# A fourth block-sum step behind two down projections, and one rounding bound ahead of later weight halves

## The chip, the cores and the metric

The kernel runs on one core of one Trainium2 chip. The metric is the device time in microseconds (us), as the median of several runs. TensorE (PE) multiplies, VectorE (DVE) and ScalarE (ACT) round and add, GpSimd (POOL) and SyncE (SP) issue the transfers from HBM.

## The reference

A trunk of two residual layers over 256 tokens with 2048 features, all in float32. Layer 0 mixes with grouped-query attention, layer 1 with a gated recurrence; each is followed by the feed-forward stage that the change is in:

```python
def swiglu(h, w_gate, w_up, w_down):
    return (jax.nn.silu(h @ w_gate) * (h @ w_up)) @ w_down
...
        x = x + mix
        x = x + swiglu(rms_norm(x, norm_ffn[i]), ffn_w_gate[i], ffn_w_up[i], ffn_w_down[i])
```

`w_gate` and `w_up` have 5632 columns, `w_down` 5632 rows.

## The kernel before

*Rounded pairs.* Each operand is held as a rounded value `hi` and the rest `lo`, and a product of two is three matmuls (`hi*hi`, `hi*lo`, `lo*hi`). Weights come in halves of 128 x 1024 numbers: two blocks of 128 rows by 512 columns. For each half `load_half` issues the transfer on SP's queue, ScalarE casts `hi` (L141), and VectorE subtracts to get `lo` (L143). `raw` has 6 buffers, `hi` and `lo` have 5 each, so the rounding can run some five halves ahead of TensorE.

*Steps.* A pair of column groups (`j` = 0 and 1, 512 columns each) is multiplied by `project_pair` with all 16 blocks of the input, taken two at a time: eight steps `n` = 0 to 7. A plain step takes a half of weights for each column group, four products each, eight in all. A *block-sum step* (`seven_forms`) does the same 2 x 2 by 2 x 2 block product with seven products, from sums and differences of the blocks (the scheme of Strassen and Winograd). It needs the sums of the weights: SP loads `wx`, POOL's queue loads `sr` with two transfers, the second adding onto the first (two `sr` buffers, fetched two block sums ahead); VectorE adds (L320, L324, L325) and takes rests (L326, L328, L329), ScalarE casts (L322, L323, L327). `wx`, `wxh` and `wxl` have one buffer each. It also needs sums of the input blocks, the *forms* of `x_forms` (L338 to L343), made once for each block pair and kept. Four products gather in PSUM tiles `pm`; after the last block-sum step of a pair `merge` (L402 to L406) folds them into two tiles `g` and `u`, to which `done` adds the accumulators (four PSUM banks, `acc`).

*Plans.* `pair_plan` takes the first steps with both columns in turn, and the rest first for column 0 and then for column 1. `THREE` = steps 1, 3 and 5 are the block sums.

*The feed-forward stage.* The 44 tiles of hidden features are cut in parts of 12, 16 and 16 (`PARTS`). In each part *units* of four tiles are made one after the other (`unit`: column group 0 is the gate, 1 the up projection), units 0 to 2, 3 to 6 and 7 to 10 of a layer; behind each part stands its down projection (`down`), two pairs of column groups, of six or eight steps, which adds into `x_tok` (L586, L594). So units 3 and 7 come right behind a down projection.

*What a unit leaves.* Its result is turned on VectorE (L862), moved by sixteen small ScalarE copies (L868) and split into `hi` and `lo` tiles (L875, L876, `split_tiles`). This work is put in the list `owed`, and `settle` takes some of it at each step of the following pair, so that the last unit of a part is turned and split during the first steps of its down projection.

*Order.* TensorE's order is as written. The other engines' order is the planner's, with three bonds: `in_line` puts weight casts (ScalarE) and rests (VectorE) in the order of the halves; `follow` puts one instruction behind another of the same engine without a semaphore; `not_after(i)` makes the rest of the fourth weight half from there come behind `i`.

Of the kernel before, what the change touches and what calls it, by code (L numbers as in the profile page):

```python
# [12 lines left out]
F32 = mybir.dt.float32  # L13
F32R = mybir.dt.float32r
AF = mybir.ActivationFunctionType
ALU = mybir.AluOpType
# [5 lines left out]
KT = D // P  # L22
# [5 lines left out]
PARTS = [12, 16, 16]  # L28
THREE, TWO, SHORT = (1, 3, 5), (2, 5), 6
READY = 6  # L30
FIRST_STEPS = (0, 1, 2, 4, 3, 6, 5, 7)
HALF = 8
WIDE = 512
# [37 lines left out]
def trunk(ctx, tc, w, out):  # L71
# [26 lines left out]
    def follow(i, j):  # L98
        tc.add_manual_dep(
            i.ins, j.ins.name,  # L100
            mybir.DependencyInfo(mybir.DependencyClass.NoSync, mybir.DependencyReason.DATA),
            reason="order",
        )
        return i


    line = {}

    def in_line(eng, i):
        if eng in line:  # L110
            if line[eng] is not None:
                follow(i, line[eng])
            line[eng] = i
        return i
# [40 lines left out]
    def pair_plan(steps, together):  # L155
        return [(n, (0, 1)) for n in steps[:together]] + [(n, (j,)) for j in range(2) for n in steps[together:]]

    def unit_seven(i):
        return THREE

    def unit_plan(i):
        steps = range(KT // 2) if i else FIRST_STEPS
        return pair_plan(steps, 1 + steps.index(unit_seven(i)[-1]))

    def down_plan(n, alone):
        if alone:
# [164 lines left out]
        fetch_next()  # L331
        return [[t[:, k, :] for t in w] for w, k in ((w1, 0), (w1, 1), (w2, 0), (w2, 1), ((xh, xl), 0), ((xh, xl), 1), ((xh, xl), 2))]

    def x_forms(h0, h1, tag):
        y = fp[0].tile([P, 8, P], F32, tag="tb", name=nm("tb"))
        for i, h in enumerate((h0, h1)):
            o, hi, lo = y[:, 2 * i : 2 * i + 2, :].rearrange("p a t -> p (a t)"), h[:, :S].bitcast(F32), h[:, S:].bitcast(F32)
            dve.tensor_tensor(o, hi, lo, ALU.add)  # L338
        for o, a, b in ((4, 1, 3), (5, 0, 4), (6, 0, 1), (7, 2, 5)):
            dve.tensor_tensor(y[:, o, :], y[:, a, :], y[:, b, :], ALU.subtract)  # L340
        t = fp[1].tile([P, 2, 4, P], F32R, tag=tag, name=nm(tag), bufs=1)
        act.copy(t[:, 0], y[:, 4:, :])
        dve.tensor_tensor(t[:, 1], y[:, 4:, :], t[:, 0].bitcast(F32), ALU.subtract)  # L343
        return [(t[:, 0, i, :], t[:, 1, i, :]) for i in range(4)]

    def project_pair(xs, forms, plan, middle, done, ready=None):
        banks = [[], []]
        begun = set()

        def bank(j, a):  # L350
            while len(banks[j]) <= a:
                banks[j].append(new_acc())
            return banks[j][a]

        def product(acc, x, wt, last=False):
            for i, (a, b) in enumerate(((x[0], wt[0]), (x[0], wt[1]), (x[1], wt[0]))):
                pe.matmul(acc, a, b, start=id(acc) not in begun, stop=last and i == 2)  # L357
                begun.add(id(acc))
            step()
            step()  # L360

        def tokens(k, a):
            return [xs[k][:, o + a * P : o + (a + 1) * P] for o in (0, S)]

        seven = [n for n, cols in plan if n in forms]
        for i, (n, cols) in enumerate(plan):
            if n in forms:
                s1, s2, s3, s4 = forms[n]
                b11, b21, t3, b22, t1, t2, t4 = seven_forms()
                settle(3)  # L370
                if n == seven[0]:
                    p1, q6, q5, q7 = (ps_m.tile([P, WIDE], F32, tag="pm", name=nm("pm")) for _ in range(4))
                last = n == seven[-1]
                product(p1, tokens(2 * n, 0), b11, last)
                product(bank(0, 0), tokens(2 * n + 1, 0), b21)
                product(bank(1, 0), s4, b22)
                product(q7, s3, t3, last)
                product(q5, s1, t1, last)
                product(q6, s2, t2, last)
                product(bank(0, 1), tokens(2 * n + 1, 1), t4)  # L380
                if last:
                    middle(p1, q5, q6, q7)
                continue
            if len(cols) == 1 and i and len(plan[i - 1][1]) == 2:
                settle(-1)
                if ready:
                    ready()
            end = n == plan[-1][0]
            for j in cols:
                half()  # L390
                if i:
                    settle(2 if len(owed) > 6 else 1)
                hi, lo = (flat(t) for t in newest["tiles"])
                for a in range(2):
                    for k in range(2):
                        product(bank(j, a), tokens(2 * n + k, a), (hi[:, k, :], lo[:, k, :]), end and k == 1)
                if end:
                    done(j, banks[j])

    def merge(p1, q5, q6, q7):  # L400
        g, u = (fp[1].tile([P, 2, WIDE], F32, tag=t, name=nm(t), bufs=1) for t in ("fg", "fu"))
        act.copy(g[:, 0, :], p1)  # L402
        dve.tensor_tensor(g[:, 1, :], q6, g[:, 0, :], ALU.subtract)
        dve.tensor_tensor(u[:, 0, :], q5, g[:, 1, :], ALU.add)
        dve.tensor_tensor(g[:, 1, :], q7, g[:, 1, :], ALU.subtract)
        dve.tensor_tensor(u[:, 1, :], u[:, 0, :], q7, ALU.subtract)  # L406
        return g, u
# [428 lines left out]
    def ffn(norm, nxt):  # L836
        coming[:] = [k for k in seven_at if taken[0] <= k < ffn_ends[taken[0] > ffn_ends[0]]]
        for _ in range(2):
            fetch_next()

        def unit(hid, hid_units, forms, parts, i):
            got = []

            def done(j, accs):
                g, u = got
                for a, acc in enumerate(accs):
                    if j == 0:
                        not_after(dve.tensor_tensor(g[:, a, :], acc, g[:, a, :], ALU.add))
                        table_act(g[:, a, :], g[:, a, :], AF.Silu, scale=norm.rt[:, a : a + 1])
                    else:  # L850
                        not_after(dve.tensor_tensor(u[:, a, :], acc, u[:, a, :], ALU.add))
                        dve.scalar_tensor_tensor(u[:, a, :], u[:, a, :], norm.rt[:, a : a + 1], g[:, a, :], ALU.mult, ALU.mult)

            project_pair(norm.xs, {n: norm.forms[n] for n in unit_seven(i)}, unit_plan(i), lambda *banks: got.extend(merge(*banks)), done)

            first = FOUR * len(hid_units)
            hid_units.append(i)
            kept = {}

            def transposes():  # L860
                kept["b"], kept["f"] = (fp[0].tile([P, 2 * FOUR, P], F32, tag=n, name=nm(n), bufs=1) for n in ("tb", "tf"))
                dve.transpose(kept["b"], got[1])  # L862

            def copies(q):
                b = kept["b"][:].rearrange("p (a i) (k t) -> p a i k t", a=2, k=FOUR)
                f = kept["f"][:].rearrange("p q (k t) -> p q k t", k=FOUR)
                for i in range(4):
                    n = act.copy(f[32 * i : 32 * i + 32, q::4, :, :], b[32 * q : 32 * q + 32, :, i, :, :])  # L868
                    follow(n, line["act"])

            def split_tiles():
                f = kept["f"][:].rearrange("p q (k t) -> p k q t", k=FOUR)
                h = act_tiles()
                hi, lo = (h[:, :, o : o + S].rearrange("p k (q t) -> p k q t", t=32) for o in (0, S))
                act.copy(hi, f)  # L875
                dve.tensor_tensor(lo, f, hi.bitcast(F32), ALU.subtract)  # L876
                hid.extend(h[:, k, :] for k in range(FOUR))
                for k, n in enumerate(THREE):
                    if n in down_seven(parts // 2, False) and first <= 2 * n < len(hid):
                        forms[n] = x_forms(hid[2 * n], hid[2 * n + 1], f"hf{k}")  # L880

            owed.extend([transposes, *(partial(copies, q) for q in range(4)), split_tiles])

        line.update(act=None, dve=None)
        for p, n in enumerate(PARTS):
            hid, units, forms = [], [], {}
            for i in range(n // FOUR):
                unit(hid, units, forms, n, sum(PARTS[:p]) // FOUR + i)
            last = p == len(PARTS) - 1
            if last and nxt is not None:  # L890
                ln_exp_tables()
            down(n, hid, forms, nxt if last else None, last and nxt is None)
        line.clear()
# [234 lines left out]
```

## Time and profile before

| | |
|---|---|
| median of 3 runs | 1956.57 us (1956.06 to 1956.72) |
| the profiled execution | 1956.03 us, its span 1954.3 us |
| PE, DVE, ACT busy in the span | 1947.8, 1742.2, 1358.4 us |
| granted TensorE clock | 1.000 |
| moved by DMA | 435.98 MB, mean 223 GB/s |

The span runs from the first to the last instruction. In the order of time a row holds the start in us from the span's start, the length in us, the engine, the line, the operation, what is written and read, and in brackets the idle time before it with what ended it. A row with "x2" holds two instructions, one behind the other; they overlap a little, so two of 1.22 take 2.35. Matmuls are pipelined: a length of 0.39 is that of one from start to end, the next begins after 0.23. In the list of waits a row holds the us in total, how often, and the longest.

### The profile page before, as it was taken

What the parts mean: (1) busy time and instruction counts of PE and PEld (TensorE: products, weight loads), DVE (VectorE), ACT (ScalarE), POOL (GpSimd) and SP (SyncE); (2) the same over time, 40 slices, a digit from 0 to 9 for tenths busy, and PEclk for the clock granted to TensorE, in tenths of its full rate; (3) what the DMA queues carried; (4) which work ended last, traced back from release to release, by engine and by line L of the source; (5) the groups of instructions that cost most, each with busy time, mean ns of one, the idle gap of its engine ahead of it and who ended that gap; (6) DMA issues with size and microseconds to landing.
All of it is one profiled execution on the core that took longest, in us unless ns stands there. A gap on an engine that the chain in (4) does not pass through costs nothing.

```text
span 1954.3 us, 27715 instructions
## 1 busy us (share of the span) xinstructions
PE 1947.8 (100%) x9635; PEld 1654.7 (85%) x9635; DVE 1742.2 (89%) x2384; ACT 1358.4 (70%) x2079; POOL 237.1 (12%) x337
## 2 busy tenths in 40 slices
PE   9999999999999999999999999999999999999999
PEld 8888888888888888888999998888888888888887
DVE  6776899998999989999878886999998999989997
ACT  6666777665677546777799896777756676567763
POOL 0011001010011100011034331011001010111010
PEclk9999999999999999999999999999999999999999
DMA  9644668687687876777655556577777787777784
GB/s 348 192 141 140 200 203 259 217 258 246 207 250 243 262 255 215 224 239 230 202 181 181 193 153 222 171 244 237 249 237 225 239 250 250 236 240 232 238 261 151
DMA packets 136939, 435.98 MB, mean 223 GB/s; under 512 B 15328, under 2 KB 16224, under 8 KB 136544
## 3 DMA queue, kind: packets, MB, share of 16 engines
q1 hardware_dynamic: 109296, 359.49, 54.1%
q0 software_dynamic: 27360, 74.72, 15.5%
q8 instruction: 75, 1.23, 0.3%
q14 instruction: 64, 0.52, 0.1%
q10 hardware_dynamic: 144, 0.02, 0.0%
HBM read 432.07 MB, written 2.10 MB: 222 GB/s over the span
## 4 chain that ended last, share of the span: by engine, by line
PE 96%; ACT 2%; DVE 1%; issue 1%; DMA 0%; SPq 0%; DVEq 0%; ACTq 0%
PE acc L357 60%; PE pm L357 13%; PE acc L273 10%; PE acc L410 3%; PE acc L411 3%; PE acc L412 3%; PE pm L273 1%; PE pm L411 1%; PE pm L410 1%; PE pm L412 1%; ACT tf L868 1%; PE pm L748 1%; PE pm L780 1%; DVE lo L143 0%; PE pm L766 0%
## 5 line engine op out<-in xcount | busy, mean ns | idle before, releaser
L143 DVE TENSOR_TENSOR lo<-raw,hi 128x1024 fp32r<-128x1024 f32 (+1 forms) x611 | 731.8, 1227 | 84.5 <-ACT hi L141 83.3
L141 ACT CAST hi<-raw 128x1024 fp32r<-128x1024 f32 (+1 forms) x611 | 622.7, 1046 | 237.9 <-PE acc L357 145.2
L357 PE MATMUL acc<-hi,xg 128*128 128x512 f32 x1892 | 604.7, 389 | 0.0
L357 PEld LDWEIGHTS acc<-hi,xg 128*128 128x128 f32 x1892 | 355.1, 188 | 73.8
L357 PE MATMUL acc<-hi,act 128*128 128x512 f32 x1258 | 402.1, 390 | 1.7 <-DVE act L876 1.4
L357 PE MATMUL acc<-lo,xg 128*128 128x512 f32 x946 | 368.0, 389 | 0.0
L357 PEld LDWEIGHTS acc<-hi,act 128*128 128x128 f32 x1258 | 236.0, 188 | 51.4 <-DVE act L876 2.3
L357 PE MATMUL acc<-lo,act 128*128 128x512 f32 x629 | 244.8, 389 | 0.0
L357 PEld LDWEIGHTS acc<-lo,xg 128*128 128x128 f32 x946 | 177.6, 188 | 36.8
L327 ACT CAST wxh<-raw 128x1024 fp32r<-128x1024 f32 x95 | 99.8, 1051 | 111.1 <-DVE raw L325 111.1
L868 ACT COPY tf<-tb 32x256 f32<-32x256 f32 x352 | 142.1, 404 | 5.5 <-DVE tb L862 1.6
L410 PE MATMUL acc<-xg,hi 128*128 128x256 f32 x512 | 144.8, 283 | 0.0
L411 PE MATMUL acc<-xg,hi 128*128 128x256 f32 x512 | 144.6, 282 | 0.0
L412 PE MATMUL acc<-xg,lo 128*128 128x256 f32 x512 | 144.4, 282 | 0.0
L357 PEld LDWEIGHTS acc<-lo,act 128*128 128x128 f32 x629 | 118.1, 188 | 23.9
L322 ACT CAST hi<-sr 128x1024 fp32r<-128x1024 f32 x95 | 99.8, 1051 | 55.4 <-PE acc L357 35.6
L323 ACT CAST wxh<-wx 128x512 fp32r<-128x512 f32 x95 | 59.0, 621 | 109.0 <-DVE wx L320 80.3
L329 DVE TENSOR_TENSOR wxl<-raw,wxh 128x1024 fp32r<-128x1024 f32 x95 | 115.3, 1213 | 7.1 <-ACT wxh L327 7.1
L326 DVE TENSOR_TENSOR lo<-sr,hi 128x1024 fp32r<-128x1024 f32 x95 | 115.7, 1218 | 0.0
L305 POOL DMA_DIRECT2D sr<-in_w_up_dram x66 | 36.7, 557 | 637.7 <-DVE lo L326 427.0
L273 PE MATMUL acc<-hi,xg 128*128 128x512 f32 x320 | 107.9, 397 | 0.0
L328 DVE TENSOR_TENSOR wxl<-wx,wxh 128x512 fp32r<-128x512 f32 x95 | 65.2, 687 | 39.3 <-ACT wxh L323 39.3
(212 smaller groups left out, 3385.8 us busy)
## 6 DMA issues: line engine op xcount, KB each, us to landing
raw<-in_w_gate_dram SPq DMA_DIRECT2D x176, 512.0 KB, 5.7
raw<-in_w_down_dram SPq DMA_DIRECT2D x147, 512.0 KB, 5.3
raw<-in_w_up_dram SPq DMA_DIRECT2D x110, 512.0 KB, 5.3
sr<-in_w_up_dram POOLq DMA_DIRECT2D x66, 512.0 KB, 4.8
raw<-in_w_in_dram SPq DMA_DIRECT2D x64, 512.0 KB, 4.3
raw<-in_w_qkv_dram SPq DMA_DIRECT2D x46, 512.0 KB, 4.6
wx<-in_w_up_dram SPq DMA_DIRECT2D x66, 256.0 KB, 4.5
sr<-in_w_up_dram POOLq DMA_DIRECT2D x66, 256.0 KB, 7.1
```

The costliest lines, as they stand in the source:

```text
L141: newest["cast"] = in_line("act", act.copy(hi[:, sl, :], raw[:, sl, :]))
L143: rest = in_line("dve", dve.tensor_tensor(lo[:, sl, :], raw[:, sl, :], hi[:, sl, :].bitcast(F32), ALU.subtract))
L273: pe.matmul(accs[a], x, wt[:, k, :], start=(k0 + k == 0 and n == 0), stop=(end and k == 1 and n == 2))
L322: in_line("act", act.copy(hi, raw))
L326: settled(in_line("dve", dve.tensor_tensor(lo, raw, hi[:].bitcast(F32), ALU.subtract)), taken[0] - 1)
L327: in_line("act", act.copy(xh[:, 1:, :], r1))
L329: in_line("dve", dve.tensor_tensor(xl[:, 1:, :], r1, xh[:, 1:, :].bitcast(F32), ALU.subtract))
L357: pe.matmul(acc, a, b, start=id(acc) not in begun, stop=last and i == 2)
L410: pe.matmul(o, hi, x[:, :S], start=start, stop=False)
L411: pe.matmul(o, hi, x[:, S:], start=False, stop=False)
L412: pe.matmul(o, lo, x[:, :S], start=False, stop=stop)
L868: n = act.copy(f[32 * i : 32 * i + 32, q::4, :, :], b[32 * q : 32 * q + 32, :, i, :, :])
```

## The change

Two things. First, for units 3 and 7 (`FOURTH`) step 7 becomes a block sum too, and the steps go in the order 1, 0, 3, 2, 5, 4, 7, 6: seven steps with both columns, then step 6 for column 0 and for column 1. The forms for step 7 are made in unit 3, when eight empty entries of `owed` have been taken, behind the newest weight rest on VectorE; unit 7 uses them again. Second, in the twelve-tile part the split of the last unit (L875 and L876 of before) is put in line with the weights' casts and rests: behind those issued before it, ahead of those issued later.

```diff
+FOURTH, FOUR_STEPS, MORE = (3, 7), (1, 0, 3, 2, 5, 4, 7, 6), 7
...
     def unit_seven(i):
-        return THREE
+        return THREE + (MORE,) if i in FOURTH else THREE
 
     def unit_plan(i):
-        steps = range(KT // 2) if i else FIRST_STEPS
-        return pair_plan(steps, 1 + steps.index(unit_seven(i)[-1]))
+        steps = FOUR_STEPS if i in FOURTH else range(KT // 2) if i else FIRST_STEPS
+        return pair_plan(steps, 1 + max(steps.index(n) for n in unit_seven(i)))
...
-    def x_forms(h0, h1, tag):
+    def x_forms(h0, h1, tag, behind=None):
...
-            dve.tensor_tensor(o, hi, lo, ALU.add)
+            made = dve.tensor_tensor(o, hi, lo, ALU.add)
+            if behind is not None:
+                follow(made, behind)
...
-            project_pair(norm.xs, {n: norm.forms[n] for n in unit_seven(i)}, unit_plan(i), lambda *banks: got.extend(merge(*banks)), done)
+            fs = {n: norm.forms.get(n) for n in unit_seven(i)}
+
+            def more():
+                fs[MORE] = norm.forms[MORE] = x_forms(norm.xs[2 * MORE], norm.xs[2 * MORE + 1], f"nf{MORE}", line["dve"])
+
+            if MORE in fs and not fs[MORE]:
+                owed.extend([lambda: None] * 8 + [more])
+            project_pair(norm.xs, fs, unit_plan(i), lambda *banks: got.extend(merge(*banks)), done)
...
-                act.copy(hi, f)
-                dve.tensor_tensor(lo, f, hi.bitcast(F32), ALU.subtract)
+                made = act.copy(hi, f), dve.tensor_tensor(lo, f, hi.bitcast(F32), ALU.subtract)
+                if parts == 2 * SHORT and len(hid) + FOUR == parts:
+                    for e, n in zip(("act", "dve"), made):
+                        in_line(e, n)
```

## The prediction

> **What bounds the kernel now.** I read the page's engine table first, then its chain, then the list of waits, then the order of time around the one wait that TensorE has in the two feed-forward stages.
>
> ```profile
> PE 1947.8 (100%) x9635; PEld 1654.7 (85%) x9635; DVE 1742.2 (89%) x2384; ACT 1358.4 (70%) x2079; POOL 237.1 (12%) x337
> PE 96%; ACT 2%; DVE 1%; issue 1%; DMA 0%; SPq 0%; DVEq 0%; ACTq 0%
> PE acc L357 <- DVE act L876: 1.4, 2, 0.7
> ```
>
> TensorE is busy for the whole span and carries 96% of the chain, so time goes only where a product is saved or a hole in its stream is closed. The third line is the only wait of the feed-forward products: two pieces, one in each layer, on the rounding rest `lo` of `split_tiles` (L876). The order of time shows the first of them, and the pace on both sides.
>
> ```profile
> 404.41 0.39 PE L357 MATMUL acc<-hi,act 128*128 128x512 f32 x1
> 404.63 0.39 PE L357 MATMUL acc<-lo,act 128*128 128x512 f32 x1
> 405.74 0.73 PE L357 MATMUL acc<-hi,act 128*128 128x512 f32 x2 [0.71 <-DVE act L876]
> 421.74 0.39 PE L357 MATMUL pm<-hi,act 128*128 128x512 f32 x1
> 473.58 0.68 PE pm L357 x3
> 1410.88 0.74 PE L357 MATMUL acc<-hi,act 128*128 128x512 f32 x2 [0.71 <-DVE act L876]
> ```
>
> The fifth line is from the chain: three matmuls, one product, take 0.68 us, so a matmul takes 0.2267 us, a half of weights (four products) 2.72 us and a block-sum step (seven products) 4.76 us in place of 5.44. From 404.41 to 421.74 there are 72 matmuls (four halves of the down projection's first column pair, two of its second), 16.32 us at that pace, and 17.33 passed. So the wait costs 1.01 us: 0.88 of hole (405.74 less 404.63 + 0.23) and 0.13 of slower restart. The second layer's row is its twin.
>
> **Part one: four steps in place of three.** Units 3 and 7 of both layers, four spots, do one product less: 4 x 0.68 = 2.72 us off a stream that has no other hole there. One rule of the Trainium skill gives another figure: "TensorE: Matmul & The Clock Gate" (Back-to-back issue gap) has 216 ns for a warm 512-column matmul, and by it the sum would be 12 x 0.216 = 2.59 us; the trace's pace decides, and nothing below uses the page's.
>
> What the step adds lies on VectorE and ScalarE. Is there room?
>
> ```profile
> 447.70:489.20 41.50, 41.50 (x185) 34.37 (x184) 36.22 (x41) 22.85 (x25) 4.25 (x6) 1.00 0.74 242
> 530.70:572.20 41.50, 41.50 (x185) 34.37 (x184) 39.67 (x51) 30.04 (x44) 4.24 (x6) 1.00 0.79 241
> 456.32 0.69 DVE L320 TENSOR_TENSOR wx<-wx,raw 128x512 f32<-128x512 f32 x1 [0.24 <-DMA wx<-in_w_up_dram]
> 460.13 1.22 DVE L329 TENSOR_TENSOR wxl<-raw,wxh 128x1024 fp32r<-128x1024 f32 x1
> 461.26 2.35 DVE L143 TENSOR_TENSOR lo<-raw,hi 128x1024 fp32r<-128x1024 f32 x2
> L338 DVE TENSOR_TENSOR tb<-xg 128x256 f32<-128x256 f32 x12 | 4.9, 418 | 0.0
> L340 DVE TENSOR_TENSOR tb<-tb 128x128 f32<-128x128 f32 x88 | 23.6, 285 | 0.1
> L343 DVE TENSOR_TENSOR nf<-tb,nf 128x512 fp32r<-128x512 f32 x6 | 4.1, 685 | 0.0
> ```
>
> The first two lines are the table by stretches (length, then PE, weight loads, DVE, ACT, POOL busy, clock, DMA share, GB/s). Unit 3 leaves VectorE idle for 5.3 us, unit 5 for 1.8 and no product waits there. A block-sum step's own sums run from L320 to L329's end, 456.32 to 461.26 = 4.94 us, after one L143 (two take 2.35, so 1.14 each in a row): 6.1 us in place of two L143s, 2.3. That is 3.8 more. The forms of x, made once a layer, in unit 3, are two L338, four L340, one L343: 2 x 0.42 + 4 x 0.285 + 0.69 = 2.7 at most. So unit 3 gets 6.5 us more VectorE work in 0.68 us less time, 1.9 us over its idle time; unit 7 3.8, under. ScalarE has 18 us free in unit 3, and takes two casts more and one of the forms.
>
> The overrun must be paid from the lead, the time by which a half is rounded before TensorE wants it. I followed VectorE's queue in the new order, 1, 0, 3, 2, 5, 4, 7, 6. At the start:
>
> ```profile
> 437.54 1.21 DVE L143 TENSOR_TENSOR lo<-raw,hi 128x1024 fp32r<-128x1024 f32 x1
> 447.78 0.69 DVE L594 TENSOR_TENSOR x_tok<-x_tok,acc 128x512 f32<-128x512 f32 x1 [0.63 <-PE acc L357]
> 449.72 1.22 DVE L326 TENSOR_TENSOR lo<-sr,hi 128x1024 fp32r<-128x1024 f32 x1
> 449.17 0.39 PE L357 MATMUL acc<-lo,xg 128*128 128x512 f32 x1
> ```
>
> Unit 3 starts at 449.17 - 7 x 0.2267 = 447.58. Its first step is now a block sum, whose eighth matmul reads L326's result, at 449.17. In this trace L326 ends at 450.94, because the bound of `not_after` (the fourth weight half behind the add) puts it behind the last add into `x_tok`, L594 at 447.78. In the new order that fourth half is step 0's second, so L326 no longer has to wait. With 437.54's L143 as the step's own, eight adds and merges of 0.6 that stand there, and L320 to L326's end (3.3), it ends near 446.8: 2.4 us of lead. From 437.54 to the end of step 7 (447.58 + 35.36 = 482.94) I count fourteen L143s (16.0), four block sums' own 4.94 (19.8), ten adds and merges (6.0) and the forms (2.7), 44.5 us of VectorE work in 45.4 us: full, with the lead kept.
>
> The tail is tighter: two halves, 5.44 us, in place of four lie between the last block sum and unit 4.
>
> ```profile
> 478.57 0.68 DVE L403 TENSOR_TENSOR fg<-pm,fg 128x512 f32<-128x512 f32 x1
> 490.49 1.22 DVE L326 TENSOR_TENSOR lo<-sr,hi 128x1024 fp32r<-128x1024 f32 x1
> 496.29 1.24 DVE L862 STREAM_TRANSPOSE tb<-fu 128x1024 f32<-128x1024 f32 x1
> 497.56 6.64 ACT L868 COPY tf<-tb 32x256 f32<-32x256 f32 x16 [0.41 <-DVE tb L862]
> 529.81 0.68 DVE L320 TENSOR_TENSOR wx<-wx,raw 128x512 f32<-128x512 f32 x1
> 534.14 1.22 DVE L326 TENSOR_TENSOR lo<-sr,hi 128x1024 fp32r<-128x1024 f32 x1
> 535.88 1.24 DVE L862 STREAM_TRANSPOSE tb<-fu 128x1024 f32<-128x1024 f32 x1
> 514.40 1.22 DVE L326 TENSOR_TENSOR lo<-sr,hi 128x1024 fp32r<-128x1024 f32 x1
> 516.49 0.39 PE L357 MATMUL acc<-lo,nf 128*128 128x512 f32 x1
> ```
>
> Unit 4 starts at 447.58 + 183 x 0.2267 = 489.06, unit 5 at 530.54. Now L326 of unit 4's first block sum ends 2.7 us after the start, in unit 5 4.8. In the new order, counted from the end of step 7: 0.4 to L403 (as at 478.57), 2.7 for the merge, 1.2 for the two gate adds, 1.1 for the L143 that `not_after` holds behind them, and L320 to L326's end as unit 5 has it (5.5): 10.9, which is 5.5 us after unit 4's start. That is 0.7 later than unit 5, against a need at 7.0: 1.5 us of lead. So the new unit 4 is run like unit 5, whose products do not wait, and I take nothing for it. If the cover goes, the first place is the last two lines: step 5's L326, 515.62, is 0.87 us ahead of its reader now.
>
> The other queues: a block sum's two POOL transfers are set off when the one before the last gives up its buffer; the nearest distance over two steps stays 20.4 us (2 x 10.2), and they land in 4.8 and 7.1 us (below). SP's `wx` load moves with its step. The banks of PSUM are taken in another order in units 3 and 7; if unit 4's second bank is the one that the first up add frees (near 1.3 us after the start, needed at 1.36), it is just in time: from 0 to 0.3 us a spot, taken as 0.
>
> ```profile
> sr<-in_w_up_dram POOLq DMA_DIRECT2D x66, 512.0 KB, 4.8
> sr<-in_w_up_dram POOLq DMA_DIRECT2D x66, 256.0 KB, 7.1
> ```
>
> **Part two: the rounding bound ahead of later halves.** L875 and L876 of the twelve-tile part's last unit go ahead of the two casts and two L143s that now stand before them.
>
> ```profile
> 400.92 2.00 ACT L141 CAST hi<-raw 128x1024 fp32r<-128x1024 f32 x2
> 402.82 1.04 ACT L875 CAST act<-tf 128x1024 fp32r<-128x1024 f32 x1
> 402.19 2.35 DVE L143 TENSOR_TENSOR lo<-raw,hi 128x1024 fp32r<-128x1024 f32 x2
> 404.46 1.22 DVE L876 TENSOR_TENSOR act<-tf,act 128x1024 fp32r<-128x1024 f32 x1
> 414.40 0.68 DVE L594 TENSOR_TENSOR x_tok<-x_tok,acc 128x512 f32<-128x512 f32 x1
> 417.27 0.68 DVE L320 TENSOR_TENSOR wx<-wx,raw 128x512 f32<-128x512 f32 x1
> 417.87 1.28 DVE L594 TENSOR_TENSOR x_tok<-x_tok,acc 128x512 f32<-128x512 f32 x2
> ```
>
> L875 can start at 400.92 and L876 at 402.19, ending 403.4, before the 404.86 at which its reader would come. The first L143 then ends at 404.55, and its reader stands at 404.63: held by 0.08 us. So the hole closes. What is late next? VectorE has no idle time from 402.19 to 419, so its later work stays where it is while TensorE comes 1.01 us earlier. The second column pair's third bank is opened 60 matmuls after 404.41, at 418.01 instead of 419.02, and that bank is freed by the L594 at 417.87, which ends at 418.55. With 0.05 us to pass on (L876 ends 405.69, its reader starts 405.74) the hole is 0.59, plus the restart's 0.13: 0.72 of 1.01 is given back. That leaves 0.29 us a layer, 0.58 in all, if that add keeps its place behind L320; if the planner sets it one place earlier, the whole 2.02.
>
> Sum: 2.72 + 0.58 = 3.30 us off the profiled execution's 1956.03, so 1952.7; the median of the runs lies 0.54 above it, which gives 1953.3.
>
> **The rivals.** *The bank comes in time.* The add is set ahead of L320, as it could be from 415 on when its bank is whole: 2.72 + 2.02 = 4.74, 1951.8. Against it: this planner put it behind L320 although it was ready 2 us before, so its own reckoning has TensorE later than the chip.
>
> *The transposes come late.* The new unit 4 keeps today's order, L862 behind two more L143s, and not unit 5's. Then L862 ends near 10 us after the start, the sixteen copies of L868 come some 2.1 us later than unit 5's, and step 5's lead of 0.9 turns into 1.2 us of waiting, at four spots: 3.3 - 4.7 = -1.4, 1958.0. For it: today's unit 4 has that order; against it: VectorE is then as late as in unit 5, which has the other.
>
> *Slower: the sums stay behind the adds.* If L326 at the start of units 3 and 7 keeps its place behind the last L594, it ends at 450.94 and TensorE waits 1.8 us at four spots: 3.3 - 7.2 = -3.9, 1960.5. It decides from some 0.8 us a spot on. The bound that put it there is gone, so little speaks for it.
>
> *The binding does nothing*, if the bound pair is held by something else: 2.72 alone, 1953.9.
>
> *The POOL transfers are starved.* With both landings twice as long (24 us and more against 20.4) a spot would wait about 4 us, and the kernel end near 1969. The issue instructions show no sign of it. The Trainium skill's "SBUF — State Buffer" (SBUF: two separate sides) has VectorE instructions that lock POOL out while it writes descriptors; no wait here shows it.
>
> **How the numbers follow.** The forecast 0.44; the bank in time 0.34; late transposes 0.11; sums behind adds 0.06; binding without effect 0.03; starved POOL 0.02. 0.2% of the time, about what a measurement of this kernel tells from no change, is 3.9 us, so faster means under 1952.66: all but 0.01 of the second case and 0.07 of the first (a bank wait that is half as long), 0.40. Slower means over 1960.5: the two bad cases and a trace of the third, 0.09. The rest, 0.51. The range runs from 1951.3, the second case less the runs' scatter of 0.5, to 1955.6, the forecast with one spot in two of the late transposes; that leaves out some 0.17.
>
> **What would show it.** In the changed profile, 9,635 - 12 matmuls; no wait on the split's rest; a new one, TensorE on the x_tok add (or none, in the second case); block sums 10.2 us apart four times in units 3 and 7; unit 4's transposes about 6 us after its start. The prediction is wrong if TensorE waits in units 3, 4, 7 or 8, or if VectorE's order around 417 has changed to the worse.

## Result and the profile after

| | before | changed |
|---|---|---|
| median (range), runs taken side by side | 1956.57 us (1955.72 to 1957.74) | 1952.11 us (1951.50 to 1953.01) |
| the profiled execution, its span | 1956.03, 1954.3 us | 1952.14, 1950.3 us |
| ratio to before, 95% interval | | 0.9978 (0.9970 to 0.9985) |

The change takes 4.46 us off, 0.23%. The forecast was 1953.3; the measured time is 0.3 us from that of the rival in which the bank comes in time (1951.8). A second series of the changed kernel, run beside two of the experiments, gave 1951.88.

Lines have moved: L141, L143, L320, L326, L357, L594, L862 and L868 of before are L142, L144, L321, L327, L360, L597, L872 and L878 after; the twelve-tile part's split, L875 and L876, has both parts on L885.

First the page's engine table and chain, and from the list of waits the one line that remains to TensorE in the feed-forward stages.

```profile
PE 1944.2 (100%) x9623; PEld 1651.8 (85%) x9623; DVE 1758.1 (90%) x2418; ACT 1362.1 (70%) x2089; POOL 242.3 (12%) x345
PE 98%; ACT 1%; DVE 0%; DMA 0%; issue 0%; SPq 0%; DVEq 0%; ACTq 0%
```

```profile
PEld acc L360 <- DVE lo L144: 0.5, 2, 0.2
```

Twelve matmuls are gone, VectorE has 15.9 us more to do, and the wait on the split is away. The list's other waits on L360 are for `gl`, outside the feed-forward stage, and stand in the list of before too. The line shown belongs to the change: a weight load that waits some 0.2 us for a rest, once a layer. The order of time around the old hole, with ScalarE and VectorE first and then TensorE:

```profile
401.50 1.04 ACT L885 CAST act<-tf 128x1024 fp32r<-128x1024 f32 x1
402.77 1.22 DVE L885 TENSOR_TENSOR act<-tf,act 128x1024 fp32r<-128x1024 f32 x1
403.91 3.49 DVE L144 TENSOR_TENSOR lo<-raw,hi 128x1024 fp32r<-128x1024 f32 x3
...
411.38 0.67 DVE L597 TENSOR_TENSOR x_tok<-x_tok,acc 128x512 f32<-128x512 f32 x1
414.99 1.27 DVE L597 TENSOR_TENSOR x_tok<-x_tok,acc 128x512 f32<-128x512 f32 x2
416.18 2.35 DVE L144 TENSOR_TENSOR lo<-raw,hi 128x1024 fp32r<-128x1024 f32 x2
418.45 0.68 DVE L321 TENSOR_TENSOR wx<-wx,raw 128x512 f32<-128x512 f32 x1
419.05 0.68 DVE L597 TENSOR_TENSOR x_tok<-x_tok,acc 128x512 f32<-128x512 f32 x1
...
405.19 0.48 PE L360 MATMUL acc<-lo,act 128*128 128x512 f32 x1
405.51 0.62 PE L360 MATMUL acc<-hi,act 128*128 128x512 f32 x2
```

The split now runs ahead of three weight rests. The first of these ends just in time: two matmuls start 0.32 us apart (405.19, 405.51) where 0.23 is the pace, so 0.09 us is lost. The third add into `x_tok` is the second of the pair at 414.99. It ends at 416.26, two weight rests and a `wx` sum ahead of where it stood, and the bank that it frees is never waited for.

At the start of unit 3 and the start of unit 4, in the order of time:

```profile
446.08 1.29 DVE L597 TENSOR_TENSOR x_tok<-x_tok,acc 128x512 f32<-128x512 f32 x2 [0.48 <-PE acc L360]
447.28 1.22 DVE L327 TENSOR_TENSOR lo<-sr,hi 128x1024 fp32r<-128x1024 f32 x1
447.24 0.39 PE L360 MATMUL pm<-hi,xg 128*128 128x512 f32 x1
448.83 0.39 PE L360 MATMUL acc<-lo,nf 128*128 128x512 f32 x1
493.81 1.24 DVE L872 STREAM_TRANSPOSE tb<-fu 128x1024 f32<-128x1024 f32 x1
```

And units 3 and 4 in the table by stretches:

```profile
447.00:487.80 40.80, 40.80 (x181) 33.75 (x180) 40.02 (x51) 23.30 (x27) 5.68 (x8) 1.00 0.87 280
487.80:529.30 41.50, 41.50 (x185) 34.37 (x184) 39.67 (x52) 30.04 (x44) 4.28 (x6) 1.00 0.76 233
```

The first half of the block sum's rests (L327) ends at 448.50, and its reader starts at 448.83: a lead of 0.33 us. By the table of stretches VectorE is busy 40.02 of unit 3's 40.80 us, and unit 3's share of DMA has gone from 0.74 to 0.87. TensorE has no hole in either stretch.

From first to last product, layer 0's feed-forward stage takes 685.38 us in this trace and layer 1's 683.29, against 687.59 and 685.58: 2.21 + 2.29 = 4.50 us. By parts that is 2.72 for the twelve matmuls and 1.78 for the hole, which was reckoned at 2.02. The span fell by 4.0 only, since the stages outside, which the change leaves alone, took 0.5 more in this execution.

### The profile page after: what moved, and what is told of

The parts are those of the page before. It is cut to its first block, busy times and chain, and to the rows that moved or that the text cites. A ratio compares the mean times of both kernels' runs of the same rounds, so it can differ in the third digit from the quotient of the medians.

```text
span 1950.3 us, 27765 instructions
## 1 busy us (share of the span) xinstructions
PE 1944.2 (100%) x9623; PEld 1651.8 (85%) x9623; DVE 1758.1 (90%) x2418; ACT 1362.1 (70%) x2089; POOL 242.3 (12%) x345
## 4 chain that ended last, share of the span: by engine, by line
PE 98%; ACT 1%; DVE 0%; DMA 0%; issue 0%; SPq 0%; DVEq 0%; ACTq 0%
PE acc L360 61%; PE pm L360 14%; PE acc L274 10%; PE acc L413 3%; PE acc L414 3%; PE acc L415 3%; PE pm L274 1%; PE pm L414 1%; PE pm L413 1%; PE pm L415 1%; PE pm L751 1%; PE pm L783 1%; PE pm L769 0%; DMA raw<-in_w_qkv_dram 0%; ACT sg L615 0%
## 5 line engine op out<-in xcount | busy, mean ns | idle before, releaser
L144 DVE TENSOR_TENSOR lo<-raw,hi 128x1024 fp32r<-128x1024 f32 (+1 forms) x607 | 726.4, 1228 | 79.8 <-ACT hi L142 79.1
L142 ACT CAST hi<-raw 128x1024 fp32r<-128x1024 f32 (+1 forms) x607 | 615.2, 1045 | 187.9 <-PE acc L360 87.9
L360 PE MATMUL acc<-hi,xg 128*128 128x512 f32 x1836 | 588.4, 389 | 0.0
L360 PEld LDWEIGHTS acc<-hi,xg 128*128 128x128 f32 x1836 | 344.6, 188 | 71.8
L360 PE MATMUL acc<-hi,act 128*128 128x512 f32 x1258 | 401.9, 390 | 0.2 <-DVE gl L938 0.2
L360 PE MATMUL acc<-lo,xg 128*128 128x512 f32 x918 | 357.1, 389 | 0.0
L360 PEld LDWEIGHTS acc<-hi,act 128*128 128x128 f32 x1258 | 236.1, 188 | 49.3 <-DVE gl L938 0.7
L360 PE MATMUL acc<-lo,act 128*128 128x512 f32 x629 | 245.0, 389 | 0.0
L360 PEld LDWEIGHTS acc<-lo,xg 128*128 128x128 f32 x918 | 172.3, 188 | 35.7
L328 ACT CAST wxh<-raw 128x1024 fp32r<-128x1024 f32 x99 | 104.1, 1051 | 124.0 <-DVE raw L326 124.0
L878 ACT COPY tf<-tb 32x256 f32<-32x256 f32 x352 | 142.1, 404 | 3.9
L360 PEld LDWEIGHTS acc<-lo,act 128*128 128x128 f32 x629 | 118.1, 188 | 24.2 <-DVE lo L144 0.5
L330 DVE TENSOR_TENSOR wxl<-raw,wxh 128x1024 fp32r<-128x1024 f32 x99 | 119.8, 1210 | 6.5 <-ACT wxh L328 6.5
L327 DVE TENSOR_TENSOR lo<-sr,hi 128x1024 fp32r<-128x1024 f32 x99 | 120.4, 1216 | 0.0
L306 POOL DMA_DIRECT2D sr<-in_w_up_dram x70 | 39.1, 558 | 605.0 <-DVE lo L327 378.2
L274 PE MATMUL acc<-hi,xg 128*128 128x512 f32 x320 | 107.6, 396 | 0.4 <-ACT hi L142 0.4
L307 POOL DMA_DIRECT2D sr<-in_w_up_dram x70 | 60.5, 865 | 316.5 <-DMA sr<-in_w_up_dram 305.3
```

The costliest lines, as they stand in the source:

```text
L142: newest["cast"] = in_line("act", act.copy(hi[:, sl, :], raw[:, sl, :]))
L144: rest = in_line("dve", dve.tensor_tensor(lo[:, sl, :], raw[:, sl, :], hi[:, sl, :].bitcast(F32), ALU.subtract))
L274: pe.matmul(accs[a], x, wt[:, k, :], start=(k0 + k == 0 and n == 0), stop=(end and k == 1 and n == 2))
L327: settled(in_line("dve", dve.tensor_tensor(lo, raw, hi[:].bitcast(F32), ALU.subtract)), taken[0] - 1)
L328: in_line("act", act.copy(xh[:, 1:, :], r1))
L330: in_line("dve", dve.tensor_tensor(xl[:, 1:, :], r1, xh[:, 1:, :].bitcast(F32), ALU.subtract))
```

## Experiments

Times are medians with their ranges; each "off" is measured against the median of the kernel before that ran on the same chip (1956.48, 1956.27, 1956.11 and 1956.38 us).

**The binding without the fourth steps.**

```diff
-FOURTH, FOUR_STEPS, MORE = (3, 7), (1, 0, 3, 2, 5, 4, 7, 6), 7
+FOURTH, FOUR_STEPS, MORE = (), (1, 0, 3, 2, 5, 4, 7, 6), 7
```

> Only the rounding bound ahead of later halves; units 3 and 7 keep three block-sum steps. Theory A (the hole closes and the third bank comes in time, because the planner now sets the third add into x_tok ahead of two weight rests and of the wx sum): 2 x (1.01 - about 0.1 of restart) = 1.8 to 2.0 us off, 1954.6 to 1954.8, no wait of TensorE on the split or on the add. Theory B (as predicted, the bank takes most of it back): 0.6 us off, 1956.0, a new wait on the add. Theory C (the binding helps only together with the fourth step): no change, 1956.6.

1954.65 us (1954.14 to 1955.54), 1.83 off; ratio 0.9991 (0.9982 to 1.0000). The list of waits has neither the split nor an add. In its order of instructions the third add, the second of this row, stands three places earlier, as in the changed kernel:

```profile
414.83 1.27 DVE L597 TENSOR_TENSOR x_tok<-x_tok,acc 128x512 f32<-128x512 f32 x2
```

So the binding moves the add by itself, and is worth 1.83 and not 0.58.

**The fourth steps without the binding.**

```diff
-                if parts == 2 * SHORT and len(hid) + FOUR == parts:
+                if False:
```

> Only the fourth block-sum step in units 3 and 7; the split of the twelve-tile part stays where the planner put it. Theory A (the two parts are independent): 4 x 0.68 = 2.72 us off, 1953.85, with the two old waits of 0.71 on the split's rest and the third add behind the wx sum again. Theory C (the fourth step lives on the lead that the binding gave): less than 2 us off, TensorE waiting at the start of unit 3, where the changed kernel has a lead of 0.3 us.

1953.71 us (1952.86 to 1954.87), 2.77 off; ratio 0.9985 (0.9976 to 0.9994). The old wait is back, with its length of before:

```profile
PE acc L360 <- DVE act L885: 1.4, 2, 0.7
```

The four spots give what the pace says (2.72). The two parts add up: 2.77 + 1.83 = 4.60 for a measured 4.46.

**The add held where the prediction had it.** After the binding, the third add is put behind the `wx` sum by hand. (The edit holds both adds of that column group; the fourth stands there in the changed kernel too.)

```diff
-        in_line("dve", dve.tensor_tensor(x, x, r1[:, 0, :], ALU.add))
+        first = in_line("dve", dve.tensor_tensor(x, x, r1[:, 0, :], ALU.add))
+        while held:
+            follow(held.pop(), first)
...
+                        if n == 2 * SHORT and c == 0 and j == 1:
+                            held.append(added)
```

> The changed kernel, but in the twelve-tile part's down projection the adds of the second column group of the first pair are held behind the next wx sum, which is the order of before. The prediction's reckoning: the third bank opens at its add's end, 0.6 us late, 0.7 with the restart, in both layers: 1.4 us slower than the changed kernel, 1953.5, and TensorE waits on x_tok with two pieces. Rival (the bank is not what binds, the lead of the weights is): no change, 1952.1.

1953.09 us (1952.81 to 1954.16), 3.39 off; ratio 0.9982 (0.9973 to 0.9991). VectorE and TensorE in this kernel's order of time, where the lines have moved (L599 is the add):

```profile
418.11 0.68 DVE L321 TENSOR_TENSOR wx<-wx,raw 128x512 f32<-128x512 f32 x1
418.71 1.28 DVE L599 TENSOR_TENSOR x_tok<-x_tok,acc 128x512 f32<-128x512 f32 x2
418.71 0.39 PE L362 MATMUL acc<-hi,act 128*128 128x512 f32 x1
419.53 0.47 PE L362 MATMUL acc<-hi,act 128*128 128x512 f32 x1 [0.43 <-ACT wxh L326]
```

The held add runs from 418.71 to 419.39, and TensorE goes on at 419.53: 0.82 between two starts, 0.59 above the pace, which is the hole that the prediction worked out (0.59). The bracket puts it down to a ScalarE cast of `wxh`; but this product reads `hi` and `act`, and the wait is not there in the changed kernel, where the add stands earlier, so the add is what ended it. The chain of reasoning was right for the order it assumed, and the order was not the one that came. The two layers' holes (0.6 each, with 0.08 at each restart) sum to 1.4 us, as expected; the medians of the two kernels differ by 1.0.

**The forms made as soon as the list allows.** The eight empty entries before the forms' making are left out.

```diff
-                owed.extend([lambda: None] * 8 + [more])
+                owed.extend([more])
```

> The changed kernel, with the forms for step 7 taken from the list at the first step of unit 3 and not after eight empty entries. Theory of leads: in the changed kernel step 0's first weight rest is ready 0.26 us before its reader; the forms' two first adds, 0.67 us, now stand before it, so TensorE waits 0.4 there, 0.5 with the restart, once a layer: 1.0 us slower, 1953.1. Rival (the place of the forms does not matter, VectorE has room): no change, 1952.1.

1953.10 us (1952.71 to 1956.39), 3.38 off; ratio 0.9983 (0.9974 to 0.9992).

```profile
449.72 0.75 DVE L339 TENSOR_TENSOR tb<-xg 128x256 f32<-128x256 f32 x2
451.56 0.39 PE L360 MATMUL acc<-hi,xg 128*128 128x512 f32 x1
452.26 0.50 PE L360 MATMUL acc<-lo,xg 128*128 128x512 f32 x1 [0.31 <-DVE lo L144]
```

0.75 us of the forms' work in unit 3's first step costs a hole of 0.47 there, in both layers, though the unit holds the same VectorE work as in the changed kernel, where nothing waits. At the start of unit 3 the lead is a few tenths and no more.

**The rests behind the last add.** At the start of units 3 and 7 the rest of the first block sum is held behind the last add, as before the change.

```diff
+        rest = in_line("dve", dve.tensor_tensor(lo, raw, hi[:].bitcast(F32), ALU.subtract))
+        settled(rest, taken[0] - 1)
+        while last_add:
+            follow(rest, last_add.pop())
...
+                        if norm is None and not end and c + j == NCOL - 1 and a == 1:
+                            last_add.append(added)
```

> The changed kernel with the rest of the first block sum's added weights (L326 of before) held behind the last add into x_tok in units 3 and 7, the price of the prediction's slower rival. By the prediction it costs 1.8 us at four spots, 7.2 in all: 1959.3. By the leads of the changed kernel it costs one add (0.6) against a lead of 0.33 us in unit 3, 0.4 with the restart, and nothing in unit 7, whose lead is 3.5: 0.8 us in all, 1952.9.

1954.31 us (1953.88 to 1956.19), 1.96 off, so 2.2 us slower than the changed kernel; ratio 0.9991 (0.9982 to 1.0000).

```profile
PE acc L363 <- DVE lo L327: 1.3, 4, 0.3
```

The first of the four in the order of time, with the adds ahead of it:

```profile
445.63 2.05 DVE L600 TENSOR_TENSOR x_tok<-x_tok,acc 128x512 f32<-128x512 f32 x3 [0.55 <-PE acc L363]
448.15 0.39 PE L363 MATMUL acc<-hi,nf 128*128 128x512 f32 x1
448.87 0.50 PE L363 MATMUL acc<-lo,nf 128*128 128x512 f32 x1 [0.33 <-DVE lo L327]
```

Four holes of 0.49, each with 0.11 of slower restart. The prediction priced this rival at 1.8 a spot, from L326's end in the old order. It is a third of that, because the three adds now run in a row (445.63, 2.05 us) and the rest comes right after them (447.60). The reckoning by the changed kernel's leads, 0.8 in all, missed too: it took unit 7's lead of 3.5 us for safe, but the last add there can start only when TensorE is done with its bank (695.86), so the rest behind it ends at 697.69, and the hole is as long as in unit 3.

**A fourth step in units 4 and 8 too.** These come after units 3 and 7, so each has a unit's transposes and copies in its first steps.

```diff
-FOURTH, FOUR_STEPS, MORE = (3, 7), (1, 0, 3, 2, 5, 4, 7, 6), 7
+FOURTH, FOUR_STEPS, MORE = (3, 4, 7, 8), (1, 0, 3, 2, 5, 4, 7, 6), 7
```

> The changed kernel with the fourth block-sum step in units 4 and 8 as well, pairs that turn and split the unit before them. If TensorE's product count alone decides: 2.72 us more off, 1949.4. Theory of leads: unit 4 of the changed kernel keeps VectorE busy for 39.7 of 41.5 us and has a lead of 0.5 us; 3.8 us more work in 0.7 us less time overruns it by 2.7 us, so TensorE waits some 2 us or more at each of four spots and the kernel is slower than the changed one: 1956 to 1960.

1979.81 us (1979.32 to 1980.12): 23.5 slower than before; ratio 1.0119 (1.0105 to 1.0133).

```profile
498.13 0.66 DVE L326 TENSOR_TENSOR raw<-raw 128x512 f32<-128x512 f32 x1
498.25 6.63 ACT L878 COPY tf<-tb 32x256 f32<-32x256 f32 x16 [2.39 <-DVE tb L872]
504.90 1.04 ACT L328 CAST wxh<-raw 128x1024 fp32r<-128x1024 f32 x1
502.22 0.39 PE L360 MATMUL pm<-wxh,nf 128*128 128x512 f32 x1
506.00 0.49 PE L360 MATMUL pm<-wxh,nf 128*128 128x512 f32 x1 [3.39 <-ACT wxh L328]
508.80 0.63 PE L360 MATMUL acc<-wxh,xg 128*128 128x512 f32 x1
509.22 0.63 PE L360 MATMUL acc<-hi,xg 128*128 128x512 f32 x1
```

The second cast of a block sum (L328) stands on ScalarE behind the sixteen copies, 6.63 us long. With block sums a step earlier TensorE comes for it at 502.45 and gets it at 506.00. The same hole stands at four spots (3.55, 3.33, 3.55 and 3.33 us with the pace taken off), each followed by one of 1.03 on the rest behind that cast. Behind these, matmuls start 0.42 to 0.43 us apart for 3 to 6 us (the last two rows), which adds 1.4 to 3.0. At the start of unit 4 a PSUM bank also comes late, by 0.87 us in one layer and 1.73 in the other. Together, less the 2.72 saved, this is the loss of 27.7 us against the changed kernel; the expectation, 1956 to 1960, had the direction but neither the place nor the size. At the four spots the wait is ScalarE's order: what the cast reads (L326) is there at 498.79, and the copies stand before it. VectorE has a share in it: the copies wait for its transpose (L872) and start at 498.25, against 496.94 in the changed kernel. The cast ahead of the copies was not tried, so how much of the loss that order alone explains is open.

**A fourth step in the down projection's second pair.** The same step was put into the second column pair of three down projections (e7) and of the two that stand ahead of unit 7 (e8). Its forms are made in that pair.

```diff
+FOUR_DOWN = ((0, 1), (1, 1), (1, 2))
...
+            four = four_down(*at, c)
+            fs = {} if alone else dict(forms)
+            if four:
+                fs[MORE] = None
+
+                def more():
+                    fs[MORE] = x_forms(xs[2 * MORE], xs[2 * MORE + 1], "hf0", line["dve"])
+
+                owed.extend([lambda: None] * 8 + [more])
```

> The changed kernel with a fourth block-sum step in three down projections too, in their second pair of column groups, where no unit is turned: both layers' first sixteen-tile part and the last part of the second layer (its forms are made in the pair, in the buffer of the first step's). If leads hold: 3 x 0.68 = 2.04 us off the changed kernel, 1950.1. If VectorE's overrun (3.8 + 2.7 us of work in 0.7 less time against 2 us of idle time and a lead of 2.6 us) comes through: waits of up to 2 us a spot, no better than 1952.1.

> As the one before, but without the last part of the second layer, behind which nothing hides the merge and the last adds. If leads hold: 1.36 us off the changed kernel, 1950.75; and if the kernel's end is what the third spot costs, this one is the better of the two.

1962.47 us (1960.99 to 1964.40), ratio 1.0031 (1.0019 to 1.0043); and 1962.76 (1958.27 to 1964.45), ratio 1.0030 (1.0020 to 1.0040). Both are slower than before by over 6 us, 10.4 and 10.7 more than the changed kernel; no expectation here had priced a bank. From e7's list of waits, its order of time, and its table by stretches:

```profile
PE acc L367 <- DVE x_tok L604: 7.4, 2, 4.0
```

```profile
696.20 0.39 PE L367 MATMUL acc<-hi,xg 128*128 128x512 f32 x1
699.93 0.76 PE L367 MATMUL acc<-hi,nf 128*128 128x512 f32 x1 [3.35 <-DVE x_tok L604]
```

```profile
700.00:706.00 6.00, 6.00 (x15) 4.72 (x16) 5.93 (x8) 0.00 (x0) 0.86 (x1) 0.54 0.80 239
706.00:712.00 6.00, 6.00 (x28) 4.91 (x28) 5.59 (x6) 3.80 (x5) 0.55 (x1) 1.00 0.53 167
```

Unit 7's second PSUM bank is waited for, once in each layer, and in the 6 us behind the hole the granted clock is 0.54, with 15 matmuls for the next stretch's 28. The trace of e8, which has not the third of these pairs, has the same two holes (3.94 and 4.14 us, against 3.51 and 4.20), so the third is not what costs. My first reading was that the banks are handed out in turn, so that the second one needed is one that the pair gives up late.

**The banks taken in the order in which they come free.** Each pair takes its banks so that the one freed first goes to the first need, the second to the second, and so on.

```diff
+        if turn:
+            need = [(0, 0), (1, 0), (0, 1), (1, 1)] if plan[0][0] in forms else FREED
+            of = dict(zip(FREED, need))
+            slots[:] = [of[s] for s in slots]
+            for s in slots:
+                bank(*s)
```

> As e7_four_down (a fourth block-sum step also in the second pair of three down projections, one per layer-part, forms made there once each), but the accumulator banks of each pair are taken in the order in which the pair before gives them up, so that the bank freed k-th is the one needed k-th. Theory (the turn of the banks cost e7 its gain): the 3.5 and 4.2 us holes at the second bank of unit 7 and the half pace behind them go; what remains is 3 x 0.68 = 2.04 us less about 0.5 us of short waits on late rests, off the 1952.1 of the changed kernel: 1950.1 to 1951.0, better than both. Rival (VectorE's order at the start of unit 7 is late whatever the bank): the wait moves to another add into x_tok or to a rest, 1 to 4 us at two spots, and the time stays at 1954 or more.

> The changed kernel with the banks taken in the order in which they are given up, and no further block sum. Theory: the changed kernel's feed-forward stage has no wait on a bank left, so nothing is to be gained: 1951.5 to 1952.5. Rival (the planner's order shifts with the banks and opens a wait of 0.5 us or more at the start of a unit): 1953 or more.

> The changed kernel itself beside these two on the same chip: 1952.1, as before, from 1951.5 to 1952.7.

With the fourth steps in the three down projections (e9): 1962.33 us (1960.20 to 1964.98), ratio 1.0031 (1.0020 to 1.0043), as bad as without it. Alone, on the changed kernel: 1952.08 (1951.73 to 1952.47), beside the changed kernel's 1951.88 (1951.37 to 1952.96). So my reading of e7 fell: the turn of the banks is worth nothing in either. What holds the bank is seen in e9's order of time, VectorE's rows first (L423 and L425 are steps of the merge, L606 adds a merged sum, L614 a bank, L337 is a weight rest):

```profile
690.80 0.68 DVE L423 TENSOR_TENSOR fg<-pm,fg 128x512 f32<-128x512 f32 x1
692.00 0.68 DVE L614 TENSOR_TENSOR x_tok<-x_tok,acc 128x512 f32<-128x512 f32 x1
695.54 0.68 DVE L425 TENSOR_TENSOR fg<-pm,fg 128x512 f32<-128x512 f32 x1
...
696.74 0.68 DVE L606 TENSOR_TENSOR x_tok<-x_tok,fu 128x512 f32<-128x512 f32 x1
697.34 1.22 DVE L337 TENSOR_TENSOR wxl<-raw,wxh 128x1024 fp32r<-128x1024 f32 x1
698.47 0.68 DVE L606 TENSOR_TENSOR x_tok<-x_tok,fg 128x512 f32<-128x512 f32 x1
...
699.68 1.27 DVE L614 TENSOR_TENSOR x_tok<-x_tok,acc 128x512 f32<-128x512 f32 x2
695.45 0.39 PE L377 MATMUL acc<-hi,xg 128*128 128x512 f32 x1
700.50 0.77 PE L377 MATMUL acc<-hi,nf 128*128 128x512 f32 x1 [4.66 <-DVE x_tok L614]
```

Between the first bank's add (692.00) and the second's (699.68) stand the end of the merge and the adds of the merged sums. In a pair with three block sums the merge comes four halves ahead of the end, 10.9 us; with a fourth step it is two halves, 5.4.

**The bank adds first.** For the two pairs ahead of unit 7, the second add of column 0 goes ahead of the merge's third step, and the merged sums' adds go behind the last bank's.

```diff
+            def add_merged(behind=None):
+                for j, t in enumerate(merged):
+                    for a in range(2):
+                        y = x_tok[:, a, c + j, :]
+                        i = dve.tensor_tensor(y, y, t[:, a, :], ALU.add)
+                        if behind is not None:
+                            follow(i, behind)
...
+                if four:
+                    if j:
+                        add_merged(added)
+                    else:
+                        follow(third[0], added)
```

> As e9_four_down_banks with the two spots ahead of unit 7 alone, and with the order of VectorE's work at the end of these two pairs changed: the accumulators of each column are added into x_tok as soon as they are whole (column 0's second add ahead of the merge's third step), and the four adds of the merged sums come last. Theory (what cost e7 and e9 is that the merge and its four adds, which a fourth step moves 5.4 us nearer to the pair's end, stand ahead of the bank adds on VectorE): unit 7's second bank is free at 695.6 instead of 700.4, the 3.3 to 4.8 us holes and the half pace behind them go, and at most 0.3 to 0.5 us a spot is left, on a merge buffer or a rest of the first block sum: 2 x 0.68 = 1.36 less 0 to 1.0 us off 1952.0: 1950.6 to 1951.7. Rival (VectorE simply has too much work at that place, in whatever order): the wait moves to the rests or the merge buffers and stays at 2 us or more a spot: 1955 or more.

1953.28 us (1951.81 to 1954.83), 3.10 off; ratio 0.9985 (0.9976 to 0.9994). Column 0's second bank add (L622) and an add of a merged sum (L612) on VectorE, and TensorE:

```profile
693.01 0.68 DVE L622 TENSOR_TENSOR x_tok<-x_tok,acc 128x512 f32<-128x512 f32 x1
...
697.14 0.69 DVE L612 TENSOR_TENSOR x_tok<-x_tok,fg 128x512 f32<-128x512 f32 x1
695.08 0.39 PE L377 MATMUL acc<-hi,xg 128*128 128x512 f32 x1
695.31 0.39 PE L377 MATMUL acc<-hi,nf 128*128 128x512 f32 x1
1701.71 0.39 PE L377 MATMUL acc<-hi,xg 128*128 128x512 f32 x1
1702.59 0.50 PE L377 MATMUL acc<-lo,xg 128*128 128x512 f32 x1 [0.49 <-DVE lo L145]
```

Column 0's second bank is free at 693.69, 1.6 us ahead of its reader (695.31), and the holes and the half clock are gone: 9.1 us off e9, with one pair fewer that has the fourth step. So VectorE's order at the end of the pair was the cause; by e8 the pair left out is not. The forecast of 1950.6 to 1951.7 did not come, though: two steps save 1.36 us, and the median is 1.2 above the changed kernel's. The trace shows holes of 0.66 (the last two rows), 0.2 and 0.2 us on weight rests at unit 7, and with each 0.1 at the restart they take back about what the two steps save. It was taken from the fastest of the eleven runs (1951.81), so what the others lost more is not seen. No version here beats the changed kernel.

## Why the prediction was right and wrong

**Part one held.** Four products less at 0.68 each are 2.72; alone they gave 2.77. By the 216 ns that the Trainium skill's "TensorE: Matmul & The Clock Gate" (Back-to-back issue gap) has for an isolated matmul, an estimate of 2.59 us, the time would differ by less than the runs scatter, so it does not tell the two apart; the pace of the rows (226.7 ns) does. The 131 ns that the same section of the Trainium skill has for a sustained stream is met by no row here. The transposes came 5.8 us after unit 4's start (493.81, against 447.24 + 180 x 0.2267 = 488.05), where unit 5's order puts them and not today's unit 4's: the rival of late transposes did not come. The POOL transfers landed in 4.8 and 7.2 us, as before. The first block sum of unit 4 had its rest at 493.29, 5.2 us after the unit's start, for the 5.5 that was reckoned.

**The step that failed** is in part two: "if that add keeps its place behind L320". The hole closed, and gave 1.78 of the 2.02 us by the trace; the forecast gave 1.44 back to a bank that the add frees late. With the binding, the planner sets the add three places earlier, so nothing is given back. The binding alone shows it in its time (1.83 and not 0.58) and in its order of instructions, and the held add shows that this add's place is what separates the two cases: 3.39 measured for the 3.30 that was summed. The reason given against the rival, that this planner had put the add late "although it was ready 2 us before", took an order as fixed whose neighbour was just being moved. Two casts and two rests fall back when the split goes ahead, and the planner schedules the whole stretch anew. Why its reckoning moved the add by three places was not traced. That the time still fell into the stated range is the rival's merit, not the forecast's: the range had been drawn down to 1951.3 to take it in, and of the 4.46 us that came the forecast's own path had 3.30.

**A term that was mis-sized without harm:** the lead at unit 3's start. The ledger had L326 end near 446.8, 2.4 us ahead. It ends at 448.50, 0.33 ahead of its reader, because two of the adds still run before it though the bound is gone. The time stayed the same, since a lead of any length costs nothing; but "full, with the lead kept" was false comfort. 0.75 us of the forms at that place opened a hole of 0.47, and holding the rest behind the last add one of 0.49.

**The smaller terms.** "The first L143 held by 0.08 us" was measured as 0.09. The restart of 0.13 is 0.08 to 0.11 in the experiments. The bank at unit 4 (0 to 0.3, taken as 0) cost nothing.

## What to carry to other kernels

Where a planner orders an engine, a change that moves one instruction reorders its neighbours: price both orders and give each its chance, rather than read the new order from the old trace. A table of busy time by stretches says that work fits, not that it is on time; what decides is the lead in front of each reader, and which few instructions stand ahead of the one that frees a bank. When a step saves 0.68 us, ask first which work it moves nearer to a deadline: that work cost holes of up to 4.8 us at a spot here, before the slower clock behind them.

## What was not expected of the hardware

A short hole and a long one did not have the same price per microsecond here. Holes of 0.5 to 0.7 us cost some 0.1 us more at the restart, and behind one of 1.73 us, in the run with units 4 and 8, the restart cost 0.08 and then the matmuls came at full pace. Behind holes of 3.3 to 4.8 us they start 0.43 us apart for 3 to 6 us (granted clock 0.54 in the 6 us quoted), which adds 1.4 to 3.0 us to the hole; in the run with units 4 and 8 the hole of 1.03 us stands between. The Trainium skill's "TensorE: Matmul & The Clock Gate" (Part 1: The HAM clock gate) has the clock fall to half after an idle window of about 3.4 us; these holes agree roughly: 1.73 us was not followed by the half pace, and the shortest that was, 3.26 us in the trace of e9, is a little below that figure; none in between was seen. Where a choice is between one wait of over 3 us and several of half a microsecond with the same sum, the short ones were cheaper here: some 0.2 us more for each us of hole, against 0.4 to 0.9.
